# Mixing layer on one core: the last row tile of the output LayerNorm, with g multiplied early and the mean subtracted by TensorE

## The chip, the cores and the metric

The kernel runs on one core of one Trainium2 chip. The metric is the device time of one execution in microseconds, taken as the median of three executions. A further execution was profiled; its trace is what the rows below come from. Five engines work side by side and meet at semaphores: TensorE (PE in the rows, with its weight loads as PEld), VectorE (DVE), ScalarE (ACT), GpSimd (POOL) and SyncE (SP), which issues most DMA transfers. ScalarE issues some transfers too.

## The reference

One layer over a sequence of 1024 rows and a model width of 1024: an adaptive LayerNorm, one input projection, two groups of attention heads, one output projection, and a LayerNorm of the residual. What the change touches is the last line alone.

```python
u = _layer_norm(x) * (1.0 + scale) + shift
h = u @ w_in                              # q, k, v, gate path of both head groups
...                                       # forgetting attention, stick-breaking attention
y = concatenate([y_fox, y_sb]) @ w_out
resid = DEEPNORM_ALPHA * x + gate * y
x = _layer_norm(resid, ln_g, ln_b)        # (resid - mu) * rsqrt(var + 1e-5) * g + b
```

The mean and the variance are taken over the 1024 columns of a row, so no row can be finished before its last column group has come out of the output projection.

## The kernel before

**Tiles and stages.** The 1024 rows are eight tiles of 128 rows, one row per partition. The kernel normalises x, projects it, runs the eight pairs of heads, and multiplies the gated head outputs by w_out (already multiplied by the gate). TensorE's order is written out by hand; on the other engines the instructions go in the order in which a scheduler put them, one behind the other on each engine. Every product that needs more than the short format's precision is done as three products of rounded parts (a part "hi" and a rest "lo"), which is why lines 915, 916 and 917 always follow each other.

**The output stage.** `OUT_ORDER` takes the row tiles as 6, 7, 4, 5, 2, 3, 0, 1. `groups(t)` cuts the 1024 columns of a tile in two halves; the last tile, tile 1, is cut in three: group 0 with columns 0 to 511, group 1 with 512 to 767 and group 2 with 768 to 1023. For each group `o_step` runs eight steps of three products into a PSUM tile (`o` in the rows), and `o_half` takes it from there. The names in its rows:

- `xr` is the tile's part of x, `r` the tile's result in SBUF, which the stores read;
- `st_b` holds the statistics of each group (line 935), `mv_b` the mean and variance joined over all groups (line 189);
- `rs_b` is the reciprocal deviation, made on GpSimd in two steps from `mv_b` (lines 191 and 192);
- `lngb` holds g and b of the LayerNorm, spread over all partitions;
- `ident` is the 128 by 128 identity in 32 bits.

**The end of a tile.** Line 934 adds alpha x to the product, line 935 takes the statistics. After the last group come the joined mean and then two passes: `first` computes (value - mean) g, `second` multiplies by the deviation and adds b. For the first seven tiles VectorE does both. For the last tile the values stay in PSUM, all first passes are done on VectorE in the order group 1, 0, 2, and the second pass is shared out: `shared` multiplies by the deviation on ScalarE and adds b on GpSimd, for group 1 and the last 96 columns of group 2; VectorE does group 0 and the first 160 columns of group 2. ScalarE's queue then stores group 0 and SP's queue stores groups 1 and 2. Each store waits for every engine that wrote its columns.

**PSUM and its order.** A PSUM tile that several engines touch is ordered by the program's semaphores: where two engines read parts of one tile, the second waits for the first. The tag `S` holds a tile of two banks for attention scores, which is free once the attention is over; the tag `ty` holds 512 columns of SBUF per buffer, used by the head outputs.

Of the kernel before, what the change touches and what calls it, by code (L numbers as in the profile page):

```python
# [8 lines left out]
F32 = mybir.dt.float32  # L9
F32R = mybir.dt.float32r  # L10
AF = mybir.ActivationFunctionType
ALU = mybir.AluOpType

P = 128
SEQ = 1024
D = 1024
# [11 lines left out]
def tile_hybrid_layer(  # L28
# [17 lines left out]
    nc = tc.nc  # L46

    cp = ctx.enter_context(tc.tile_pool(name="const", bufs=1))
    sb = ctx.enter_context(tc.tile_pool(name="sb", bufs=1))
# [3 lines left out]
    def big(tag, bufs, name, dt=F32, shape=None):  # L53
        return sb.tile(shape or [P, 1024], dt, tag=tag, bufs=bufs, name=name)

    def att_tile(name, dt=F32):
        return big("att", 6, name, dt)
# [13 lines left out]
    def s_tile(name):  # L71
        return ps.tile([P, 2, 512], F32, tag="S", bufs=1, name=name)
# [17 lines left out]
    ident = cp.tile([P, P], F32, tag="ident", name="ident")  # L90
# [90 lines left out]
    for kt in range(NB):  # L181
        nc.tensor.matmul(sc_all[:, kt // 4, kt % 4 * P:][:, :P], sc[:, kt:kt + 1].to_broadcast([P, P]), ident,
                         start=True, stop=True)
# [3 lines left out]
    def ln_finish(st, name):  # L187
        mv = sb.tile([P, 2], F32, tag="mv", bufs=3, name=f"mv_{name}")
        nc.vector.bn_aggr(mv, st)
        rs = sb.tile([P, 2], F32, tag="rs", bufs=3, name=f"rs_{name}")  # L190
        nc.gpsimd.tensor_scalar_add(rs[:, 0:1], mv[:, 1:2], EPS)
        powed[0] = nc.gpsimd.tensor_tensor(rs[:, 0:1], rs[:, 0:1], mhalf, op=ALU.pow)
        return mv, rs
# [29 lines left out]
    def in_turn(make, *args):  # L223
        with after(*turn_of):
            turn_of[:] = [make(*args)]
        return turn_of[0]
# [456 lines left out]
    for kb in range(NB):  # L683
        last = kb == NB - 1
# [17 lines left out]
        else:  # L702
# [3 lines left out]
            rest = in_turn(u_rest, kb + 1)  # L706
# [107 lines left out]
    for kb in range(NB):  # L814
# [9 lines left out]
        if kb < len(evacs):  # L824
            n, h = evacs[kb]
# [5 lines left out]
    first = nc.scalar.copy(held[:, :512], acc1[0])  # L831
    last = nc.vector.tensor_copy(held[:, 512:], acc1[1])
# [46 lines left out]
    lgb = {}  # L879
# [21 lines left out]
    def groups(t):  # L901
        return ((0, 512), (512, 768), (768, 1024)) if t == OUT_ORDER[-1] else ((0, 512), (512, 1024))
# [18 lines left out]
    def o_half(t, h):  # L921
        ts_ = slice(t * P, (t + 1) * P)
        s = slice(*groups(t)[h])
        ng = len(groups(t))
        if h == 0:
            xr = big("k", 4, f"xr_{t}")
            nc.sync.dma_start(xr, x[ts_, :])
            res[t] = (att_tile(f"r_{t}"), xr, sb.tile([P, 3, 6], F32, tag="st", bufs=3, name=f"st_b{t}")[:, :ng, :])
        r, xr, st = res[t]
        last = t == OUT_ORDER[-1]  # L930

        acc = o_acc[t, h][:, :s.stop - s.start]
        to = acc if last else r[:, s]
        nc.vector.scalar_tensor_tensor(to, xr[:, s], ALPHA, acc, op0=ALU.mult, op1=ALU.add)
        nc.vector.bn_stats(st[:, h, :], to)
        if h == ng - 1:
            mv, rs = ln_finish(st, f"b{t}")
            cuts = [slice(*g) for g in groups(t)]
            mid = [o_acc[t, j][:, :c.stop - c.start] if last else r[:, c] for j, c in enumerate(cuts)]

            def first(j):
                nc.vector.scalar_tensor_tensor(mid[j], mid[j], mv[:, 0:1], lgb[0][:, 0, cuts[j]],
                                               op0=ALU.subtract, op1=ALU.mult)

            def second(c, m):
                nc.vector.scalar_tensor_tensor(r[:, c], m, rs[:, 0:1], lgb[0][:, 1, c], op0=ALU.mult, op1=ALU.add)

            def shared(c, m):
                nc.scalar.activation(r[:, c], m, AF.Copy, scale=rs[:, 0:1])
                nc.gpsimd.tensor_tensor(r[:, c], r[:, c], lgb[0][:, 1, c], op=ALU.add)  # L950

            if not last:
                for j in range(2):
                    first(j)
                    second(cuts[j], mid[j])
                    nc.sync.dma_start(out[ts_, cuts[j]], r[:, cuts[j]])
                return
            for j in (1, 0, 2):
                first(j)
            shared(cuts[1], mid[1])  # L960
            c = cuts[2]
            cut = c.stop - 96
            shared(slice(cut, c.stop), mid[2][:, cut - c.start:])
            second(cuts[0], mid[0])
            second(slice(c.start, cut), mid[2][:, :cut - c.start])
            nc.scalar.dma_start(out[ts_, cuts[0]], r[:, cuts[0]])
            rest = slice(cuts[1].start, c.stop)
            nc.sync.dma_start(out[ts_, rest], r[:, rest])

    def gen_out_first(t):  # L970
# [5 lines left out]
    def gen_out_last(t):  # L976
        for h in range(2):
            o_step(t, h, NPAIR - 1)
            o_half(t, h)
            yield  # L980

    def gen_out(t):
        for h in range(len(groups(t))):
            for pr in range(NPAIR):
                o_step(t, h, pr)
                if pr == NPAIR - 1:
                    o_half(t, h)
                yield
# [186 lines left out]
```

## Time and profile before

| what | value |
|---|---|
| median of 3 executions | 682.38 us (682.34 to 682.41) |
| profiled execution | 682.39 us, span of its trace 680.6 us |
| TensorE busy | 670.2 us (98% of the span) |
| VectorE busy | 484.8 us (71%) |
| GpSimd busy | 406.1 us (60%) |
| ScalarE busy | 380.1 us (56%) |
| granted TensorE clock, mean | 0.997 of full speed |
| the last 7.1 us of the span | from the end of TensorE's last product at 673.49 to 680.6, TensorE idle |

How to read it: the span runs from the first to the last event of the trace, and the execution's own time is 1.8 us longer. The times of rows are in microseconds from the span's start. A busy share is a mean over stages with different limits; what a change of the last tile can do is read from the last microseconds alone. The ends of products are modelled, since TensorE works on several at once: a product's row can be longer than the distance to the next one.

### The profile page before, as it was taken

How to read it: one execution, taken by the hardware profiler on the slowest of the kernel's cores; microseconds unless marked ns; L12 is line 12 of the kernel's file. 1: busy time of each engine (PE TensorE's matmuls, PEld its weight loads, DVE VectorE, ACT ScalarE, POOL GpSimd, SP SyncE). 2: the span in 40 equal slices, each digit the busy share in tenths (PEclk: the TensorE clock that was granted, in tenths of full speed). 3: DMA queues.
4: the chain of work that ended last, by engine and by line, in shares of the span. 5: the costliest groups of instructions: out<-in, count | busy, mean ns of one | idle time of the engine just before them, and what ended most of it. 6: DMA issues, size and time to landing. Idle time of an engine off the chain costs nothing.

```text
span 680.6 us, 11191 instructions
## 1 busy us (share of the span) xinstructions
PE 670.2 (98%) x3713; PEld 571.7 (84%) x3713; DVE 484.8 (71%) x996; ACT 380.1 (56%) x857; POOL 406.1 (60%) x530
## 2 busy tenths in 40 slices
PE   8999999999999999999999999999999999999995
PEld 5788898888997888889988888889988888888885
DVE  6787779868666777777676675766676777885645
ACT  6567368756566666666665564656565766521000
POOL 5550279756357656566369778786795365655412
PEclk9999999999999999999999999999999999999998
DMA  9983432112102122122134454363352297153301
GB/s 332 401 309 117 140 76 77 41 29 59 34 11 66 41 54 56 40 54 55 32 109 144 147 165 156 106 192 118 118 178 59 60 361 299 59 178 105 119 32 62
DMA packets 46472, 81.54 MB, mean 120 GB/s; under 512 B 5264, under 2 KB 20176, under 8 KB 46416
## 3 DMA queue, kind: packets, MB, share of 16 engines
q1 hardware_dynamic: 44832, 76.37, 34.6%
q10 hardware_dynamic: 1584, 4.47, 2.1%
q8 instruction: 29, 0.48, 0.3%
q14 instruction: 27, 0.22, 0.1%
HBM read 60.34 MB, written 16.29 MB: 113 GB/s over the span
## 4 chain that ended last, share of the span: by engine, by line
PE 94%; DVE 2%; ACT 1%; POOL 1%; issue 0%; POOLq 0%; DVEq 0%
PE m L297 10%; PE m L298 10%; PE m L299 10%; PE pv L531 10%; PE T L514 9%; PE S L463 5%; PE S L462 5%; PE o L917 4%; PE o L915 4%; PE o L916 4%; PE v L355 4%; PE v L357 4%; PE v L356 4%; PE st_late L623 1%; PE st_q L623 1%; PE sc_all L176 1%
## 5 line engine op out<-in xcount | busy, mean ns | idle before, releaser
L517 DVE TENSOR_TENSOR pt<-T,pt 128x512 fp32r<-128x512 f32 (+2 forms) x192 | 102.6, 553 | 43.2 <-ACT pt L516 41.7
L516 ACT CAST pt<-T 128x512 fp32r<-128x512 f32 (+2 forms) x192 | 88.7, 478 | 64.3 <-PE T L514 62.5
L297 PE MATMUL m<-uh,whi 128*128 128x512 f32 x304 | 123.4, 406 | 0.0
L299 PE MATMUL m<-uh,wlo 128*128 128x512 f32 x304 | 119.8, 394 | 0.0
L298 PE MATMUL m<-ul,whi 128*128 128x512 f32 x304 | 119.6, 394 | 0.0
L497 POOL TENSOR_TENSOR be<-be,kp 128x127 f32<-128x127 f32 (+3 forms) x64 | 79.0, 1235 | 37.4 <-DVE kp L495 25.8
L491 DVE TENSOR_TENSOR_SCAN kp<-kp,floor 128x512 f32<-128x512 f32 (+2 forms) x64 | 65.0, 1016 | 25.5 <-ACT kp L484 24.4
L531 PE MATMUL pv<-pt,v 128*128 128x512 f32 x320 | 82.8, 388 | 0.0
L478 POOL TENSOR_SCALAR a<-a,l 128x1024 f32<-128x1024 f32 (+3 forms) x64 | 48.4, 757 | 36.5 <-DVE l L476 27.8
L462 PE MATMUL S<-k,q 128*128 128x512 f32 (+5 forms) x192 | 68.8, 360 | 0.3 <-ACT be L486 0.3
L299 PEld LDWEIGHTS m<-uh,wlo 128*128 128x128 f32 x304 | 57.1, 188 | 13.7
L475 ACT ACTIVATE a<-a,nm 128x1024 f32<-128x1024 f32 (+3 forms) x64 | 49.8, 778 | 29.2 <-DVE nm L470 28.8
L297 PEld LDWEIGHTS m<-uh,whi 128*128 128x128 f32 x304 | 57.2, 188 | 10.1 <-PE T L514 0.3
L463 PE MATMUL S<-kl,qz 128*128 128x512 f32 (+5 forms) x192 | 65.3, 341 | 0.0
L298 PEld LDWEIGHTS m<-ul,whi 128*128 128x128 f32 x304 | 57.3, 188 | 9.0
L531 PEld LDWEIGHTS pv<-pt,v 128*128 128x128 f32 x320 | 55.4, 189 | 9.1
L547 POOL TENSOR_TENSOR ty<-ty,sg 64x256 f32<-64x256 f32 x64 | 47.0, 734 | 24.0 <-issue 11.0
L470 DVE CUSTOM_DVE_ANT_0 a<-S,fb 128x1024 f32<-128x1024 f32 (+3 forms) x64 | 48.2, 753 | 16.8 <-PE S L463 13.1
L436 ACT CAST qz<-q 64x128 fp32r<-64x128 f32 x128 | 37.3, 296 | 33.9 <-PE S L463 32.7
L355 PE MATMUL v<-whi_v,uh 128*128 128x256 f32 (+1 forms) x192 | 54.7, 285 | 0.0
L357 PE MATMUL v<-wlo_v,uh 128*128 128x256 f32 (+1 forms) x192 | 54.2, 282 | 0.0
L484 ACT ACTIVATE kp<-S 128x128 f32<-128x128 f32 (+3 forms) x64 | 42.0, 656 | 21.5 <-PE S L463 20.2
(289 smaller groups left out, 1622.6 us busy)
## 6 DMA issues: line engine op xcount, KB each, us to landing
raw<-in_w_qkg_dram SPq DMA_DIRECT2D x38, 256.0 KB, 2.8
wss<-in_w_ss_dram SPq DMA_DIRECT2D x16, 512.0 KB, 8.5
x<-in_x_dram SPq DMA_DIRECT2D x8, 512.0 KB, 6.6
k<-k SPq DMA_DIRECT2D x32, 128.0 KB, 2.3
wg<-in_w_gate_dram SPq DMA_DIRECT2D x8, 512.0 KB, 4.6
raw_o<-in_w_out_dram SPq DMA_DIRECT2D x16, 256.0 KB, 2.9
fb<-f_dr ACTq DMA_DIRECT2D x8, 512.0 KB, 4.4
wo_dr<-whi_o SPq DMA_DIRECT2D x16, 256.0 KB, 2.1
```

The source lines that it names most:

```text
L297: nc.tensor.matmul(acc, hi[:, c], u_hi[kt][:, s], start=(kt == 0), stop=False)
L298: nc.tensor.matmul(acc, hi[:, c], u_lo[kt][:, s], start=False, stop=False)
L299: nc.tensor.matmul(acc, lo[:, c], u_hi[kt][:, s], start=False, stop=(kt == NB - 1))
L355: nc.tensor.matmul(acc[:, :n], u_hi[kt][:, ts_], hi[:, s], start=(kt == 0), stop=False)
L357: nc.tensor.matmul(acc[:, :n], u_hi[kt][:, ts_], lo[:, s], start=False, stop=(kt == NB - 1))
L462: nc.tensor.matmul(S[:, s, :w], qst[p][h][:, qs], kst[p][h][:, ks], start=True, stop=False)
L463: nc.tensor.matmul(S[:, s, :w], z, klo[p][:, ks], start=False, stop=True)
L491: last_dve = nc.vector.tensor_tensor_scan(rv, rv, floor[:, :ke - lo], initial=0.0, op0=ALU.mult, op1=ALU.max)
L497: nc.gpsimd.tensor_tensor(be[:, :ke - 1], be[:, :ke - 1], kp[:, 1:ke], op=ALU.mult)
L516: nc.scalar.copy(hi[:, :n, qo:qo + P], t3)
L517: lows[:] = [nc.vector.tensor_tensor(lo[:, :n, qo:qo + P], t3, hi.bitcast(F32)[:, :n, qo:qo + P], op=ALU.subtract)]
L531: nc.tensor.matmul(acc2[:, :, q0:], vt[p][:, kb, h * P:(h + 1) * P], pt[:, :, q0:], start=(kb == 0), stop=(kb == last))
```

## The change

In the last tile alone, three things are different.

1. After the statistics of groups 0 and 1, VectorE at once writes value times g to `r` (line 937 of the changed kernel), before the mean is known.
2. TensorE multiplies these columns of `r` by the identity into `o_whole`, a tile of the two free banks of tag `S` (line 963). When the mean is there, VectorE makes a diagonal matrix of minus the mean, 128 by 128, in a buffer of tag `ty` (line 965), and TensorE adds the product of this diagonal and g to the same banks (line 967). The banks then hold value g - mean g, which is the result of `first`. For group 2 `first` stays on VectorE.
3. The second pass is shared out otherwise. `shared` takes group 1 in two pieces of 128 columns; VectorE does groups 0 and 2 whole.

```diff
         nc.vector.bn_stats(st[:, h, :], to)
+        if last and h < ng - 1:
+            nc.vector.tensor_tensor(r[:, s], to, lgb[0][:, 0, s], op=ALU.mult)
         if h == ng - 1:
             mv, rs = ln_finish(st, f"b{t}")
...
-            for j in (1, 0, 2):
-                first(j)
-            shared(cuts[1], mid[1])
-            c = cuts[2]
-            cut = c.stop - 96
-            shared(slice(cut, c.stop), mid[2][:, cut - c.start:])
+            whole = s_tile("o_whole")
+            mid[:2] = [whole[:, j, :c.stop - c.start] for j, c in enumerate(cuts[:2])]
+            for j in (0, 1):
+                nc.tensor.matmul(mid[j], ident, r[:, cuts[j]], start=True, stop=False)
+            dm = sb.tile([P, 512], F32, tag="ty", bufs=2, name="mean_diag")[:, :P]
+            nc.vector.tensor_scalar(dm, ident, mv[:, 0:1], -1.0, op0=ALU.mult, op1=ALU.mult)
+            for j in (0, 1):
+                nc.tensor.matmul(mid[j], dm, lgb[0][:, 0, cuts[j]], start=False, stop=True)
+            first(2)
+            for c in (slice(512, 640), slice(640, 768)):
+                shared(c, mid[1][:, c.start - cuts[1].start:c.stop - cuts[1].start])
             second(cuts[0], mid[0])
-            second(slice(c.start, cut), mid[2][:, :cut - c.start])
+            second(cuts[2], mid[2])
             nc.scalar.dma_start(out[ts_, cuts[0]], r[:, cuts[0]])
-            rest = slice(cuts[1].start, c.stop)
+            rest = slice(cuts[1].start, D)
             nc.sync.dma_start(out[ts_, rest], r[:, rest])
```

How the instructions stand on the engines is shown by the built programs. In their rows the operand left of the arrow is written, those right of it are read; the bracket names the semaphores waited for: `PE_49` is raised by TensorE, `DVE_49` by VectorE, `Activation_49` by ScalarE, `Pool_49` by GpSimd. `o_0`, `o_1` and `o_2` are the PSUM tiles of the three groups.

VectorE at the last tile, from group 1 to its end, before:

```order
L934 SCALAR_TENSOR_TENSOR o_1_7705<-xr_7699,o_1_7705 128x256 [waits PE_49]
L935 BN_STATS st_b_7702<-o_1_7705 128x6 [waits DVE_49]
L934 SCALAR_TENSOR_TENSOR o_2_7732<-xr_7699,o_2_7732 128x256 [waits PE_49]
L935 BN_STATS st_b_7702<-o_2_7732 128x6 [waits DVE_49]
L189 BN_AGGR mv_b_7759<-st_b_7702 128x2 [waits DVE_49]
L942 SCALAR_TENSOR_TENSOR o_1_7705<-o_1_7705,mv_b_7759,lngb 128x256 [waits DVE_49]
L942 SCALAR_TENSOR_TENSOR o_0_7674<-o_0_7674,mv_b_7759,lngb 128x512
L942 SCALAR_TENSOR_TENSOR o_2_7732<-o_2_7732,mv_b_7759,lngb 128x256
L946 SCALAR_TENSOR_TENSOR r_7701<-o_0_7674,rs_b_7761,lngb 128x512 [waits DVE_49,Pool_49]
L946 SCALAR_TENSOR_TENSOR r_7701<-o_2_7732,rs_b_7761,lngb 128x160 [waits Activation_49]
```

And now, from group 0's multiplication on:

```order
L937 TENSOR_TENSOR r_7701<-o_0_7674,lngb 128x512
L934 SCALAR_TENSOR_TENSOR o_1_7706<-xr_7699,o_1_7706 128x256 [waits PE_49]
L935 BN_STATS st_b_7702<-o_1_7706 128x6 [waits DVE_49]
L937 TENSOR_TENSOR r_7701<-o_1_7706,lngb 128x256
L934 SCALAR_TENSOR_TENSOR o_2_7734<-xr_7699,o_2_7734 128x256 [waits PE_49]
L935 BN_STATS st_b_7702<-o_2_7734 128x6 [waits DVE_49]
L189 BN_AGGR mv_b_7761<-st_b_7702 128x2 [waits DVE_49]
L965 TENSOR_SCALAR mean_diag<-ident,mv_b_7761 128x128 [waits DVE_49]
L944 SCALAR_TENSOR_TENSOR o_2_7734<-o_2_7734,mv_b_7761,lngb 128x256
L948 SCALAR_TENSOR_TENSOR r_7701<-o_2_7734,rs_b_7763,lngb 128x256 [waits DVE_49,Pool_49]
L948 SCALAR_TENSOR_TENSOR r_7701<-o_whole,rs_b_7763,lngb 128x512 [waits PE_49,Activation_49]
```

The second pass of group 0 moved behind that of group 2 and now waits for TensorE and for ScalarE; two multiplications stand ahead of the last group's statistics.

TensorE at its end, now (before, the program ended with line 917):

```order
L917 MATMUL o_2_7734<-wol_6735,y7h 128x256
L963 MATMUL o_whole<-r_7701,ident 128x512 [waits DVE_49]
L963 MATMUL o_whole<-r_7701,ident 128x256 [waits DVE_49]
L967 MATMUL o_whole<-lngb,mean_diag 128x512 [waits DVE_49]
L967 MATMUL o_whole<-lngb,mean_diag 128x256
```

Four 32-bit products came in behind the last step of the projection; in the built program TensorE's semaphore is raised once for the four, by the last.

ScalarE at its end, before:

```order
L949 ACTIVATE r_7701<-o_1_7705,rs_b_7761 128x256 [waits DVE_49,Pool_49]
L949 ACTIVATE r_7701<-o_2_7732,rs_b_7761 128x96 [waits DVE_49]
L966 DMA out_dram<-r_7701 128x512 [waits DMAHW7_49,DVE_49]
```

And now:

```order
L951 ACTIVATE r_7701<-o_whole,rs_b_7763 128x128 [waits DVE_49,PE_49,Pool_49]
L951 ACTIVATE r_7701<-o_whole,rs_b_7763 128x128
L973 DMA out_dram<-r_7701 128x512 [waits DMAHW0_49,DVE_49]
```

ScalarE's first piece now waits for TensorE too, and its store still waits for VectorE's second pass of group 0. On every engine the rows ahead of the last tile stand in the same order as before, with other line numbers.

## The prediction

> **What bounds the kernel now.** I read the page first, for the engine that carries the span.
>
> ```profile
> PE 94%; DVE 2%; ACT 1%; POOL 1%; issue 0%; POOLq 0%; DVEq 0%
> ```
>
> The chain that ended last is TensorE for 94% of it. The change touches no product of that part: it begins at the last row tile, so the question is what comes after TensorE's last product. I read that stretch in order of time (columns: start, duration, engine, line, operation, operands; in brackets the idle time before it and what ended it).
>
> ```profile
> 668.57 0.70 DVE L935 BATCH_NORM_STATS2 st_b<-o 128x6 f32<-128x512 f32 x1
> 670.69 0.43 DVE L934 SCALAR_TENSOR_TENSOR o<-xr,o 128x256 f32<-128x256 f32 x1 [1.42 <-PE o L917]
> 671.15 0.43 DVE L935 BATCH_NORM_STATS2 st_b<-o 128x6 f32<-128x256 f32 x1
> 673.21 0.28 PE L917 MATMUL o<-wol,y7h 128*128 128x256 f32 x1
> 673.52 0.43 DVE L934 SCALAR_TENSOR_TENSOR o<-xr,o 128x256 f32<-128x256 f32 x1 [1.94 <-PE o L917]
> 673.99 0.43 DVE L935 BATCH_NORM_STATS2 st_b<-o 128x6 f32<-128x256 f32 x1
> 674.46 0.24 DVE L189 BATCH_NORM_AGGREGATE mv_b<-st_b 128x2 f32<-128x18 f32 x1
> 674.73 1.54 DVE L942 SCALAR_TENSOR_TENSOR o<-o,mv_b,lngb 128x256 f32<-128x256 f32 x3
> 675.09 0.56 POOL L192 TENSOR_TENSOR rs_b<-rs_b,mhalf 128x1 f32<-128x1 f32 x1
> 675.68 0.96 ACT L949 ACTIVATE r<-o,rs_b 128x256 f32<-128x256 f32 x2 [47.03 <-POOL rs_b L192]
> 676.18 1.03 DVE L946 SCALAR_TENSOR_TENSOR r<-o,rs_b,lngb 128x512 f32<-128x512 f32 x2
> 676.23 1.07 POOL L950 TENSOR_TENSOR r<-r,lngb 128x256 f32<-128x256 f32 x2 [0.58 <-ACT r L949]
> 676.95 0.34 ACTq L966 DMA_DIRECT2D out_dram<-r  x1
> 677.33 0.33 SPq L968 DMA_DIRECT2D out_dram<-r  x1
> ```
>
> Three branches leave the mean at 674.70. GpSimd makes the reciprocal deviation by 675.65. VectorE runs three first passes until 676.27. ScalarE and GpSimd share the second pass with VectorE. ScalarE starts as soon as the deviation is there, because the first pass of group 1 went first and was done by 675.22. The two stores are issued at 676.95 and 677.33. The second waits for GpSimd, whose adds end at 677.30, while VectorE is done at 677.21: the branches are level within 0.1 us. A saving on VectorE alone is therefore worth nothing here.
>
> What follows the stores is shown by the windows (length, five busy times, granted clock, DMA share, GB/s).
>
> ```profile
> 677.70:678.00 0.30, 0.00 (x0) 0.00 (x0) 0.00 (x0) 0.00 (x0) 0.00 (x0) 0.50 0.64 246
> 678.00:678.30 0.30, 0.00 (x0) 0.00 (x0) 0.00 (x0) 0.00 (x0) 0.00 (x0) 0.50 0.98 375
> 678.90:679.20 0.30, 0.00 (x0) 0.00 (x0) 0.00 (x0) 0.00 (x0) 0.00 (x0) 0.50 0.78 294
> 679.20:679.50 0.30, 0.00 (x0) 0.00 (x0) 0.00 (x0) 0.00 (x0) 0.00 (x0) 0.50 0.01 0
> ```
>
> Data starts near 677.80, 0.85 us after the first issue, and fills the queues until 679.13 (1.33 us for both stores). The span ends 1.47 us later, at 680.6. The first store alone already has a share of 0.98, so the second adds to a queue that is full.
>
> **The change part by part.** Removed: two of the three first passes after the mean. Added on VectorE ahead of the mean: two multiplications by g, after the statistics of groups 0 and 1. They read PSUM with one more operand like line 934, so 0.70 us (its 512 wide form ran 0.70 too) and 0.43 us. The first would run from 669.3 to 670.0 and the second from 671.6 to 672.0. VectorE is idle there: 1.42 us before 670.69 and 1.94 us before 673.52. So they cost nothing; without that cover they would cost 1.13 us in front of the mean.
>
> Added on TensorE: two copies by the identity and two products by the diagonal, each 512 and 256 wide, all 32-bit on both sides. The nearest rows are the warm-up products of line 176, equal in type and width.
>
> ```profile
> 9.92 1.02 PE L176 MATMUL st_q<-ident 128*128 128x512 f32 x2
> 10.78 0.27 PE L242 MATMUL xT_early<-ident,x 128*128 128x128 f32 x1
> 12.07 0.60 PE L176 MATMUL st_q<-ident 128*128 128x256 f32 x2
> 12.51 0.27 PE L242 MATMUL xT_early<-ident,x 128*128 128x128 f32 x1
> ```
>
> One such product is two records. The 512 wide one holds the array 0.86 us (9.92 to 10.78), the 256 wide 0.44 us, and the last result comes 0.16 us after that. The copies go in behind line 917 at 673.33 and are through at 674.63, with results by 674.79. The mean is there at 674.70 and its diagonal later still, so TensorE's idle time hides them; without that cover they cost 1.30 us.
>
> The diagonal is new on the path. It is one 128 wide operation with a scalar per row, from SBUF to SBUF.
>
> ```profile
> L757 DVE TENSOR_SCALAR gate<-wg,sc 128x512 f32<-128x512 f32 x2 | 0.9, 480 | 0.0
> L217 DVE TENSOR_SCALAR x<-x,mv_a,rs_a 128x1024 f32<-128x1024 f32 x2 | 1.6, 814 | 0.6 <-POOL rs_a L192 0.5
> L842 DVE COPY floor<-ident 128x128 f32<-128x128 f32 x1 | 0.3, 289 | 0.0
> ```
>
> A line through 480 and 814 ns gives 0.23 us at 128; the copy of this size, into PSUM, took 0.29. I take 0.25: the diagonal is ready at 674.98.
>
> What a hand-over and a product after a wait cost is read here, the first three from the chain in order of time, the others from TensorE's first microseconds.
>
> ```profile
> 673.50 0.02 issue
> 674.70 0.08 issue
> 676.17 0.07 issue
> 13.67 0.50 PE L623 MATMUL st_q<-uh,whi_stk 128*128 128x512 f32 x1 [0.34 <-ACT uh L255]
> 14.01 0.40 PE L623 MATMUL st_k<-uh,whi_stk 128*128 128x512 f32 x1
> 14.24 0.39 PE L623 MATMUL st_g<-uh,whi_stk 128*128 128x512 f32 x1
> ```
>
> VectorE to GpSimd took 0.08, TensorE to VectorE 0.02; I take 0.07 to TensorE. The first product after a wait was followed 0.34 us later, the next 0.23 later, so 0.11 us of weight load is exposed. The products of the mean then run from 675.05: 0.11 + 0.86 + 0.60 = 1.57, to 676.62. No engine can start between the two, since the built program signals only behind the last: ScalarE and VectorE both wait for TensorE there.
>
> Here the stall is: ScalarE starts at 676.64 in place of 675.68, 0.96 us late, although the deviation was ready at 675.65 as before. The pieces that follow are shorter. Their prices lie between these groups:
>
> ```profile
> L949 ACT ACTIVATE r<-o,rs_b 128x256 f32<-128x256 f32 x1 | 0.5, 475 | 47.0 <-POOL rs_b L192 47.0
> L949 ACT ACTIVATE r<-o,rs_b 128x96 f32<-128x96 f32 x1 | 0.3, 342 | 0.1
> L950 POOL TENSOR_TENSOR r<-r,lngb 128x256 f32<-128x256 f32 x1 | 0.7, 725 | 0.6 <-ACT r L949 0.6
> L950 POOL TENSOR_TENSOR r<-r,lngb 128x96 f32<-128x96 f32 x1 | 0.4, 392 | 0.0
> L946 DVE SCALAR_TENSOR_TENSOR r<-o,rs_b,lngb 128x512 f32<-128x512 f32 x1 | 0.7, 743 | 0.0
> L942 DVE SCALAR_TENSOR_TENSOR o<-o,mv_b,lngb 128x256 f32<-128x256 f32 x2 | 1.0, 488 | 0.0
> ```
>
> At 128 wide that is 0.37 on ScalarE and 0.46 on GpSimd. ScalarE ends its first piece at 677.01 and its second, a little overlapped, at 677.33. GpSimd runs from 677.08; two pieces less the 0.05 by which the pair of before overlapped (0.725 + 0.392 against 1.07) are 0.87, to 677.95. SP issues its store at 677.98.
>
> VectorE is later still. It does the first and second pass of group 2 by about 676.2 (0.49 each, after 674.98), and then holds a new wait. The order shows its 512 wide second pass waiting for TensorE and for ScalarE: both of ScalarE's pieces read the same tile and stand ahead of it. It starts at 677.39 and ends at 678.13. Queued behind it is ScalarE's store of group 0, at 678.16; before, that store was the first to go, at 676.95.
>
> The sum: the first issue moves from 676.95 to 677.98, 1.03 us; the second from 677.33 to 678.16, 0.83 us. Both stores overlap as before, and one alone already fills the queues, so the end follows the first issue: 677.98 + 0.85 + 1.33 + 1.47 = 681.63 against 680.6, or +1.03 us. The page named Trainium Kernel Development and Optimization, in the Trainium skill, section Key Constraints, says that transfers issued from SP and ScalarE run on the same 16 DMA engines and interleave; the trace agrees, with a share of 0.98 for one store. By that rule the end follows the first issue, +1.03; if each store had a landing time of its own, it would follow the second, +0.83.
>
> The profiled execution took 682.39 (span 680.6 and 1.8 around it), 0.01 above the median of 682.38. The forecast is 682.39 + 1.03, so 683.4.
>
> Bounds: with the diagonal at 0.23, a hand-over of 0.02, no exposed load, ScalarE at 0.27 and GpSimd at 0.39 a piece, SP issues at 677.52: +0.57, 682.95. With 0.29, 0.08, a load of 0.19, no overlap of the two products (1.62), 0.40 on ScalarE and 0.48 on GpSimd, it issues at 678.41: +1.46, 683.85. I lie nearer the upper bound, by the rows of equal shape.
>
> **The rivals.** *The slow clock (slower).* If TensorE's clock falls to a half before the products of the mean, their 1.30 us of streaming double: +1.3 more, 684.7. These rows speak of it:
>
> ```profile
> 675.00:676.00 1.00, 0.00 (x0) 0.00 (x0) 1.00 (x3) 0.32 (x1) 0.56 (x2) 1.00 0.00 0
> 676.00:677.00 1.00, 0.00 (x0) 0.00 (x0) 1.00 (x3) 0.50 (x2) 0.77 (x2) 0.64 0.00 0
> ```
>
> The clock fell to 0.50 inside the second, about 2.8 us after the last product. After the change the gap is only 674.79 to 675.05, so it should stay up; it decides if the fall comes before 676. Falling at 676.3, as before, it doubles only the last 0.3 us. The Trainium skill, TensorE: Matmul & The Clock Gate, section What's actually happening, has the clock at a half after an idle window of about 3.4 us that runs free of the kernel. By that rule the products run at full clock and the sum stands at 683.4; the trace, with its fall after 2.8 us, neither needs nor excludes the window.
>
> *Cheap products.* If the 32-bit products cost as little as those of line 623 (0.23 us a 512 wide one, half of that a 256 wide), the chain shortens by 0.86 + 0.44 - 0.35 = 0.95 us and the end by as much: +0.1, 682.5. Against it stands line 176 with the same types on both sides. Even so nothing is gained, for ScalarE cannot start before 675.68 and VectorE still waits behind it.
>
> *A gain.* To end 1.4 us earlier, the first store would have to go at 675.6, before the deviation exists. I find no mechanism; what is left is chance of a different placement elsewhere, and the order shows no moved instruction ahead of the last tile.
>
> **How the numbers follow.** About 0.2%, 1.36 us, is what a measurement of this kernel can tell from no change, so slower begins at 683.74. The forecast has 73%, and its own range, 682.95 to 683.85, has about 11 of these above 683.74. The slow clock has 12%, cheap products 12%, a gain 3%. That makes faster 3%, same 62 + 12 = 74%, slower 11 + 12 = 23%. The range is 682.5 to 684.0: it takes in the cheap products and the bounds, and leaves out the gain and most of the slow clock.
>
> **What would show it.** Right: four 32-bit products behind line 917, the last two ending near 676.6; ScalarE's first piece at 676.6 released by TensorE and not by the deviation; VectorE's 512 wide second pass released by ScalarE at 677.4; the first store from SP near 678.0 and ScalarE's near 678.2; the clock at 1.00 to 676. Wrong: a mean product of 512 columns under 0.5 us, ScalarE released by GpSimd, VectorE's 512 wide pass beginning with ScalarE's, or the mean itself later than 674.7, which would mean that the multiplications or copies are not hidden.

## The result, and the profile after

The changed kernel takes 683.57 us against 682.43 us (medians of 18 runs each): a ratio of 1.0016, with a 95% interval of 1.0009 to 1.0023. It is 1.14 us slower: the interval does not hold 1. The median lies within the 0.2% (1.36 us) that the prediction set as the bound for no change; the interval's upper end lies a little beyond it. The forecast was 683.4. Of the 18 executions, which took 683.27 to 684.07 us, five spent 2.24 to 2.38 us outside the span in place of 1.8, and the profiled one (684.04) is among them, so what follows is read inside the trace.

The end of the changed kernel in order of time (start, duration, engine, line, operation, operands; in brackets the idle time before and what ended it):

```profile
669.46 0.67 DVE L937 TENSOR_TENSOR r<-o,lngb 128x512 f32<-128x512 f32 x1
670.96 0.43 DVE L934 SCALAR_TENSOR_TENSOR o<-xr,o 128x256 f32<-128x256 f32 x1 [0.83 <-PE o L917]
671.77 0.41 DVE L937 TENSOR_TENSOR r<-o,lngb 128x256 f32<-128x256 f32 x1
...
673.48 0.28 PE L917 MATMUL o<-wol,y7h 128*128 128x256 f32 x1
673.60 1.45 PE L963 MATMUL o_whole<-r,ident 128*128 128x512 f32 x4
673.80 0.43 DVE L934 SCALAR_TENSOR_TENSOR o<-xr,o 128x256 f32<-128x256 f32 x1 [1.62 <-PE o L917]
674.73 0.24 DVE L189 BATCH_NORM_AGGREGATE mv_b<-st_b 128x2 f32<-128x18 f32 x1
675.00 0.29 DVE L965 TENSOR_SCALAR mean_diag<-ident,mv_b 128x128 f32<-128x128 f32 x1
675.05 0.31 POOL L191 TENSOR_SCALAR rs_b<-mv_b 128x1 f32<-128x1 f32 x1 [8.98 <-DVE mv_b L189]
675.34 1.56 PE L967 MATMUL o_whole<-lngb,mean_diag 128*128 128x512 f32 x4 [0.29 <-DVE mean_diag L965]
675.45 0.56 POOL L192 TENSOR_TENSOR rs_b<-rs_b,mhalf 128x1 f32<-128x1 f32 x1
676.05 0.48 DVE L948 SCALAR_TENSOR_TENSOR r<-o,rs_b,lngb 128x256 f32<-128x256 f32 x1 [0.36 <-POOL rs_b L192]
676.99 0.62 ACT L951 ACTIVATE r<-o_whole,rs_b 128x128 f32<-128x128 f32 x2 [48.06 <-PE o_whole L967]
677.43 0.87 POOL L952 TENSOR_TENSOR r<-r,lngb 128x128 f32<-128x128 f32 x2 [1.42 <-ACT r L951]
677.65 0.75 DVE L948 SCALAR_TENSOR_TENSOR r<-o_whole,rs_b,lngb 128x512 f32<-128x512 f32 x1 [1.11 <-ACT r L951]
678.32 0.33 SPq L975 DMA_DIRECT2D out_dram<-r  x1
678.43 0.35 ACTq L973 DMA_DIRECT2D out_dram<-r  x1
```

Read the brackets. ScalarE's first piece is released by TensorE at 676.99, although the deviation (line 192) was there at 676.01. VectorE's 512 wide pass sits idle for 1.11 us and is released by ScalarE. Both waits are new.

In this trace TensorE's last projection product begins at 673.48, in that of before at 673.21, with the same instructions up to there. Over all the kernels below it lies between 673.01 and 673.48, though TensorE's order up to there is the same in all of them. The lowest value belongs to a kernel that has the early multiplications (early work alone), so the shift is not theirs. So positions are compared below as distances from the end of the joined mean (line 189), which is 674.97 here and 674.70 before; the mean itself comes 1.49 us after the start of the last product in both. By that measure ScalarE starts at 2.02 us after the mean (0.98 before), the first store goes at 3.35 (2.25) and the second at 3.46 (2.63).

The data of the two stores, in windows (length, five busy times, granted clock, DMA share, GB/s):

```profile
678.90:679.20 0.30, 0.00 (x0) 0.00 (x0) 0.00 (x0) 0.00 (x0) 0.00 (x0) 1.00 0.12 48
679.20:679.50 0.30, 0.00 (x0) 0.00 (x0) 0.00 (x0) 0.00 (x0) 0.00 (x0) 1.00 1.04 410
...
680.10:680.40 0.30, 0.00 (x0) 0.00 (x0) 0.00 (x0) 0.00 (x0) 0.00 (x0) 1.00 1.08 423
680.40:680.70 0.30, 0.00 (x0) 0.00 (x0) 0.00 (x0) 0.00 (x0) 0.00 (x0) 1.00 0.22 75
```

It runs from about 679.16 to 680.47, 0.84 us behind the first issue, without a gap, and the span ends at 681.8. From the mean to the end of the data it is 5.50 us, against 4.43 before: 1.07 us of the 1.14.

### The profile page after: what moved, and what is told of

It reads as the page before. It is cut to its first block, busy times and chain, and to the rows that moved or that the text cites. A ratio compares the mean times of both kernels' runs of the same rounds, so it can differ in the third digit from the quotient of the medians.

```text
span 681.8 us, 11209 instructions
## 1 busy us (share of the span) xinstructions
PE 672.6 (99%) x3721; PEld 572.8 (84%) x3721; DVE 485.3 (71%) x997; ACT 380.0 (56%) x857; POOL 405.8 (60%) x530
## 4 chain that ended last, share of the span: by engine, by line
PE 93%; DVE 3%; ACT 1%; DMA 1%; POOL 1%; issue 0%; SPq 0%; DVEq 0%; ACTq 0%; POOLq 0%
PE m L297 10%; PE m L298 10%; PE m L299 10%; PE pv L531 10%; PE T L514 9%; PE S L463 5%; PE S L462 5%; PE o L917 4%; PE o L916 4%; PE o L915 4%; PE v L355 4%; PE v L357 4%; PE v L356 4%; PE st_late L623 1%; PE st_q L623 1%; DMA x<-in_x_dram 1%
```

## The experiments

**One table for all.** Columns 2 to 4 are microseconds after the end of the joined mean in each kernel's own trace, worked out from its rows as above. "End" is what a count of the stores makes of columns 3 and 4, as a difference to the kernel before: the data ends 2.18 us after the first store (0.85 to the first data, 1.33 for both stores) or 1.52 us after the second (0.85 and half of 1.33), whichever is later, less the 4.43 of before. The first way of counting is the prediction's; the second is not in it, and was first used in the expectation for the two-tile kernel. "Measured" is the difference of the medians to the kernel before in the same comparison.

| kernel | ScalarE starts | first store | second store | end | measured |
|---|---|---|---|---|---|
| before | 0.98 | 2.25 | 2.63 | 0 | 0 |
| the change | 2.02 | 3.35 | 3.46 | +1.10 | +1.14 |
| mean products twice | 3.31 | 4.65 | 4.75 | +2.40 | +2.37 |
| two tiles | 2.02 | 2.32 | 3.35 | +0.44 | +0.52 |
| two tiles, group 1 first | 1.17 | 2.50 | 2.75 | +0.25 | +0.17 |
| rounded products | 1.14 | 2.48 | 2.59 | +0.23 | +0.14 |
| sharing alone | 0.98 | 2.26 | 2.68 | +0.01 | +0.01 |
| early work alone | 0.99 | 2.26 | 2.63 | +0.01 | 0.00 |
| rounded, two tiles, group 1 first | 1.15 | 2.32 | 2.48 | +0.07 | -0.02 |
| the same, VectorE's group 0 first | 1.14 | 1.95 | 2.48 | -0.30 | -0.35 |
| the same, diagonal from PSUM | 0.98 | 1.95 | 2.37 | -0.30 | -0.33 |
| the same, diagonal by ScalarE | 1.02 | 2.06 | 2.49 | -0.19 | -0.22 |

**Mean products twice.** Is the price that of TensorE's products on the path? Doubling them should add their streaming time, once.

```diff
-nc.vector.tensor_scalar(dm, ident, mv[:, 0:1], -1.0, ...)
+nc.vector.tensor_scalar(dm, ident, mv[:, 0:1], -0.5, ...)
+for j in (0, 1):
+    nc.tensor.matmul(mid[j], dm, lgb[0][:, 0, cuts[j]], start=False, stop=False)
 for j in (0, 1):
     nc.tensor.matmul(mid[j], dm, lgb[0][:, 0, cuts[j]], start=False, stop=True)
```

> The changed kernel with its two mean products done twice, each time with a diagonal of minus half the mean; the result is the same. Theory A (the 32-bit mean products stand on the path, and the stores follow them): the products stream 0.86 + 0.44 us more, ScalarE's first piece starts 1.30 us later after the joined mean (3.32 us in place of 2.02) and the time is 683.57 + 1.30 = 684.9 us. Theory B (the loss comes from the new sharing of the second pass, or from early work that is not hidden, and the products have cover): no change from 683.6. Theory C (the slow clock is what matters): a longer stretch of products, +2.6 us, 686.2.

684.64 us against 682.27 (ratio 1.0034, 1.0021 to 1.0046). The end in order of time:

```profile
674.45 0.24 DVE L189 BATCH_NORM_AGGREGATE mv_b<-st_b 128x2 f32<-128x18 f32 x1
...
676.46 1.45 PE L969 MATMUL o_whole<-lngb,mean_diag 128*128 128x512 f32 x4
678.00 0.63 ACT L951 ACTIVATE r<-o_whole,rs_b 128x128 f32<-128x128 f32 x2 [49.35 <-PE o_whole L969]
...
679.34 0.33 SPq L977 DMA_DIRECT2D out_dram<-r  x1
```

ScalarE starts 3.31 us after the mean, 1.29 later than in the change, and the time against the kernel before goes from +1.14 to +2.37. The products are on the path at their full length. No cover is left, and no effect of the clock appears: it is granted at 1.00 in every microsecond from 674 to 679.

**Two tiles.** Takes away VectorE's wait for ScalarE by giving group 1 a PSUM tile of its own. VectorE then does not wait for group 1's product either, since group 0's signals by itself; ScalarE still stands behind both products.

```diff
-mid[:2] = [whole[:, j, :c.stop - c.start] for j, c in enumerate(cuts[:2])]
+mid[:2] = [whole[:, 0, :512], pv_tile("o_one")[:, :256]]
```

> The changed kernel with the sums of groups 0 and 1 in two PSUM tiles in place of one, so that VectorE's 512 wide second pass no longer waits for ScalarE, and group 0's product signals by itself. Theory A (the products on the path, and VectorE's new wait delaying the store of group 0): ScalarE still starts 2.02 us after the joined mean and SP's store still goes at 3.35, but VectorE's 512 wide pass starts at about 1.5 in place of 2.68 and ScalarE's store goes at about 2.3 in place of 3.46. The data then ends 0.6 us earlier: 683.0 us, +0.5 to the kernel before. A rival, that VectorE's wait alone is the loss: back to 682.4. Another, that only the last store issued counts and the queues have room: the later store moves from 3.46 to 3.35, so 683.5.

682.79 us against 682.27 (1.0008, 1.0000 to 1.0017). In order of time, and then the windows of the stores:

```profile
674.33 0.24 DVE L189 BATCH_NORM_AGGREGATE mv_b<-st_b 128x2 f32<-128x18 f32 x1
...
675.91 0.59 PE L967 MATMUL o_one<-lngb,mean_diag 128*128 128x256 f32 x2
...
676.11 0.75 DVE L948 SCALAR_TENSOR_TENSOR r<-o_whole,rs_b,lngb 128x512 f32<-128x512 f32 x1
676.59 0.63 ACT L951 ACTIVATE r<-o_one,rs_b 128x128 f32<-128x128 f32 x2 [48.06 <-PE o_one L967]
676.89 0.34 ACTq L973 DMA_DIRECT2D out_dram<-r  x1
...
677.92 0.33 SPq L975 DMA_DIRECT2D out_dram<-r  x1
```

```profile
678.00:678.30 0.30, 0.00 (x0) 0.00 (x0) 0.00 (x0) 0.00 (x0) 0.00 (x0) 1.00 1.00 389
678.30:678.60 0.30, 0.00 (x0) 0.00 (x0) 0.00 (x0) 0.00 (x0) 0.00 (x0) 1.00 0.41 150
```

VectorE's pass no longer waits for ScalarE; group 0 is stored at 2.32 us in place of 3.46, and 0.6 us of the loss are gone. One store alone has a share of 1.00 in the first window, and it falls to 0.41 in the second: the first store's data is through before the second's begins, so from here the end hangs on the second store. That is where the two ways of counting the end part: 2.32 + 2.18 = 4.50, 3.35 + 1.52 = 4.87, and the measured +0.52 goes with 4.87. So the two waits of VectorE were worth 0.6 us of the 1.14. Nearly all of it belongs to the one for ScalarE: group 1's product ends at 676.50 by its row, so an estimate with that wait alone puts VectorE's start near 676.52, the first store at 2.73 and the end at +0.48 by the table's count, in place of +0.44. The rest stands with ScalarE's late start.

**Two tiles, group 1 first.** Of that rest, how much is the order of the products?

```diff
-for j in (0, 1):
+for j in (1, 0):
     nc.tensor.matmul(mid[j], dm, lgb[0][:, 0, cuts[j]], start=False, stop=True)
```

> As the two-tile kernel, with the mean product of group 1 ahead of that of group 0. Theory A: ScalarE no longer waits for the 512 wide product; it starts when the deviation is there, 1.05 us after the joined mean in place of 2.02, SP's store goes at 2.4 in place of 3.35, VectorE's 512 wide pass starts at 1.95 and ScalarE's store goes at 2.7. Against the kernel before (2.25 and 2.63) that is +0.1 to +0.2: 682.6 us. If the products cost less than 0.3 us of the path, the order would move nothing: 683.0 as with two tiles alone.

682.44 us against 682.27 (1.0002, 0.9993 to 1.0011).

```profile
674.30 0.24 DVE L189 BATCH_NORM_AGGREGATE mv_b<-st_b 128x2 f32<-128x18 f32 x1
...
675.71 0.63 ACT L951 ACTIVATE r<-o_one,rs_b 128x128 f32<-128x128 f32 x2 [47.21 <-PE o_one L967]
...
676.51 0.75 DVE L948 SCALAR_TENSOR_TENSOR r<-o_whole,rs_b,lngb 128x512 f32<-128x512 f32 x1 [0.41 <-PE o_whole L967]
677.04 0.33 SPq L975 DMA_DIRECT2D out_dram<-r  x1
```

ScalarE starts at 1.17 us, 0.85 earlier, nearly the 0.86 of the 512 wide product that no longer stands ahead of it. Of the 0.52 us left of the loss, 0.35 go with the order; the other 0.17 the interval does not tell from nothing. The expectation put ScalarE's start at 1.05; the product of group 1 still releases it, 0.13 after the deviation.

**Rounded products.** The change as it is, with one tile and both of its waits, but with cheap mean products. Left out is precision: g and the diagonal are rounded to the short format and no rest is added, so the mean's part is less exact. VectorE makes the rounded diagonal with another operation, which takes 0.35 us in place of 0.29.

```diff
+nc.scalar.activation(g_neg[0][:, 0, :], lgb[0][:, 0, :], AF.Copy, scale=-1.0)   # once, at group 0
...
-dm = sb.tile([P, 512], F32, tag="ty", ...)
-nc.vector.tensor_scalar(dm, ident, mv[:, 0:1], -1.0, op0=ALU.mult, op1=ALU.mult)
+dm = sb.tile([P, 512], F32R, tag="ty", ...)
+nc.vector.scalar_tensor_tensor(dm, ident, mv[:, 0:1], ident, op0=ALU.mult, op1=ALU.mult)
...
-    nc.tensor.matmul(mid[j], dm, lgb[0][:, 0, cuts[j]], start=False, stop=True)
+    nc.tensor.matmul(mid[j], dm, g_neg[0][:, 0, cuts[j]], start=False, stop=True)
```

> The changed kernel with the mean products in the rounded 32-bit format that the projection uses; what is left out is the precision of the mean's part: g (negated, copied once by ScalarE while it idles) and the diagonal are rounded, and no rest is added. One PSUM tile and VectorE's wait for ScalarE stay. Theory A (the price is the passes of full 32-bit products): 0.23 + 0.12 us of streaming in place of 0.86 + 0.44, so ScalarE starts when the deviation is there, 1.05 us after the joined mean in place of 2.02, the stores go at 2.4 and 2.5, and the time is +0.1 to +0.2 on the kernel before: 682.6 us. The rival, that VectorE's wait for ScalarE and the sharing are the loss: little gain, 683.2 to 683.6.

682.41 us against 682.27 (1.0001, 0.9992 to 1.0010).

```profile
675.10 0.62 PE L970 MATMUL o_whole<-g_neg,mean_diag 128*128 128x512 f32 x2 [0.36 <-DVE mean_diag L968]
...
675.80 0.63 ACT L954 ACTIVATE r<-o_whole,rs_b 128x128 f32<-128x128 f32 x2 [47.19 <-POOL rs_b L192]
...
676.46 0.75 DVE L951 SCALAR_TENSOR_TENSOR r<-o_whole,rs_b,lngb 128x512 f32<-128x512 f32 x1 [0.18 <-ACT r L954]
```

The two products take 0.62 us in place of 1.56, and ScalarE is released by the deviation again. With VectorE's wait and the sharing unchanged, the loss falls from 1.14 to 0.14 us, which the interval does not tell from nothing. VectorE still waits for ScalarE, but 0.18 us in place of 1.11. So most of what that wait cost came of ScalarE being late: it passed the products' price on to the store of group 0.

**Sharing alone, and early work alone.** Two parts of the change on the kernel before: the new sharing of the second pass; and the early multiplications with the copies by the identity, whose results are not used.

```diff
 # sharing alone
-shared(cuts[1], mid[1])
-shared(slice(cut, c.stop), mid[2][:, cut - c.start:])
+for c in (slice(512, 640), slice(640, 768)):
+    shared(c, mid[1][:, c.start - cuts[1].start:c.stop - cuts[1].start])
 second(cuts[0], mid[0])
-second(slice(c.start, cut), mid[2][:, :cut - c.start])
+second(cuts[2], mid[2])
 # early work alone
+if last and h < ng - 1:
+    nc.vector.tensor_tensor(r[:, s], to, lgb[0][:, 0, s], op=ALU.mult)
...
+whole = s_tile("o_whole")
+for j, c in enumerate(cuts[:2]):
+    nc.tensor.matmul(whole[:, j, :c.stop - c.start], ident, r[:, c], start=True, stop=True)
```

> The kernel before with only the new sharing of the second pass: ScalarE and GpSimd take group 1 in two pieces of 128 columns, VectorE takes groups 0 and 2 whole; the three first passes stay on VectorE. Theory A (the sharing is no part of the loss): GpSimd ends earlier and VectorE later, at 2.8 us after the joined mean in place of 2.5; the store of group 0 goes at 2.25 as before, that of SP at 2.83 in place of 2.63, and because the first store fills the queues the end stays: 682.4 us, within 0.2. Theory B (the sharing is the loss): +0.5 us or more. If the end follows the later store: +0.2.

> The kernel before with the early multiplications by g and the copies by the identity added, their results unused; the first and second passes stay as before. Theory A (this work lies in idle time): the joined mean comes as long after the last projection product as before (1.49 us from its start), the stores as before, 682.4 us within 0.2. Theory B (it is not hidden): up to 1.1 us more ahead of the mean if the multiplications are in the way, up to 1.3 if the copies are.

682.26 us with the sharing (1.0001, 0.9992 to 1.0009) and 682.25 with the early work (1.0000, 0.9991 to 1.0009), against 682.25. With the sharing the stores go at 2.26 and 2.68, as before within 0.05; VectorE's pair of second passes took 1.13 us in place of the 1.23 that the prediction's rows of 512 and 256 columns add up to (743 and 488 ns), so even the later store hardly moves. The sharing:

```profile
674.34 0.24 DVE L189 BATCH_NORM_AGGREGATE mv_b<-st_b 128x2 f32<-128x18 f32 x1
...
676.84 0.34 ACTq L964 DMA_DIRECT2D out_dram<-r  x1
677.26 0.33 SPq L966 DMA_DIRECT2D out_dram<-r  x1
```

With the early work, from its order of time:

```profile
673.01 0.28 PE L917 MATMUL o<-wol,y7h 128*128 128x256 f32 x1
673.13 1.45 PE L962 MATMUL o_whole<-r,ident 128*128 128x512 f32 x4
673.33 0.43 DVE L934 SCALAR_TENSOR_TENSOR o<-xr,o 128x256 f32<-128x256 f32 x1 [1.62 <-PE o L917]
...
674.26 0.24 DVE L189 BATCH_NORM_AGGREGATE mv_b<-st_b 128x2 f32<-128x18 f32 x1
```

The mean ends 1.49 us after the start of the last product, the same as without that work: the multiplications fall into VectorE's idle time, of which 1.62 us are still left, and the copies run beside the statistics. Neither part costs anything that the traces or the medians show.

**The parts put together.** If the products and the order of the stores are all that matters, cheap products with two tiles and group 1 first should come level with the kernel before, and VectorE doing group 0 ahead of group 2 should get ahead of it. Both have the rounded precision of the mean's part.

```diff
 # on top of the rounded products
-mid[:2] = [whole[:, j, :c.stop - c.start] for j, c in enumerate(cuts[:2])]
+mid[:2] = [whole[:, 0, :512], pv_tile("o_one")[:, :256]]
...                                          # mean products in the order (1, 0)
 # group 0 first
-second(cuts[0], mid[0])
-second(cuts[2], mid[2])
+with after(second(cuts[0], mid[0])):
+    second(cuts[2], mid[2])
```

> Rounded mean products, two PSUM tiles, group 1 first; the mean's part has the rounded precision. Theory A: ScalarE starts with the deviation at 1.05 us after the joined mean, SP's store goes at 2.4; VectorE does group 2 first, then group 0 from about 1.55 to 2.3, and ScalarE's store goes at 2.3. Against 2.25 and 2.63 before: the end follows the first store, so +0.1: 682.4 to 682.5 us. If the end follows the last store: -0.2.

> As the kernel with rounded products, two tiles and group 1 first, but VectorE's second pass of group 0 ahead of that of group 2. Theory A (the end follows the first store as long as it alone fills the queues): group 0 is done 1.85 us after the joined mean and stored at 1.87 in place of 2.25 before; SP's store goes at 2.4. The data ends 0.4 us earlier than before: 682.0 us. If the end follows the last store: 682.2. If the rounded products are still on the path: 682.6.

682.23 us (1.0000, 0.9991 to 1.0008) and 681.90 us (0.9995, 0.9986 to 1.0004) against 682.25. The second is the fastest kernel of the study, 0.35 us below the kernel before. Its interval holds 1, but its slowest execution (682.00) is below the fastest of the 33 of the kernel before beside it (682.05). Its order of time:

```profile
674.38 0.24 DVE L189 BATCH_NORM_AGGREGATE mv_b<-st_b 128x2 f32<-128x18 f32 x1
674.65 0.35 DVE L969 SCALAR_TENSOR_TENSOR mean_diag<-ident,mv_b 128x128 fp32r<-128x128 f32 x1
674.71 0.38 POOL L191 TENSOR_SCALAR rs_b<-mv_b 128x1 f32<-128x1 f32 x1 [8.98 <-DVE mv_b L189]
...
675.79 0.75 DVE L951 SCALAR_TENSOR_TENSOR r<-o_whole,rs_b,lngb 128x512 f32<-128x512 f32 x1 [0.38 <-POOL rs_b L192]
...
676.57 0.34 ACTq L977 DMA_DIRECT2D out_dram<-r  x1
677.10 0.33 SPq L979 DMA_DIRECT2D out_dram<-r  x1
```

Its second store goes as late as that of the kernel with VectorE's group 2 first (2.48 in both), and only the first moved, from 2.32 to 1.95: the time followed it by 0.33 us.

**Where the diagonal is made.** In these traces GpSimd's step of line 191 is longer than before (0.31 in the change, 0.38 here, 0.22 before). The row of the kernel before:

```profile
674.78 0.22 POOL L191 TENSOR_SCALAR rs_b<-mv_b 128x1 f32<-128x1 f32 x1 [8.98 <-DVE mv_b L189]
```

Two more kernels, on top of the last, ask whether VectorE's operation beside it is the reason.

```diff
 # diagonal from PSUM
+nc.scalar.copy(ident_ps[0], ident)          # once, at group 0
-nc.vector.scalar_tensor_tensor(dm, ident, mv[:, 0:1], ident, ...)
+nc.vector.scalar_tensor_tensor(dm, ident_ps[0], mv[:, 0:1], ident, ...)
 # diagonal by ScalarE
-nc.vector.scalar_tensor_tensor(dm, ident, mv[:, 0:1], ident, ...)
+nc.scalar.activation(dm, ident, AF.Copy, scale=mv[:, 0:1])
```

> The kernel with rounded products, two tiles and group 0 first, but VectorE makes the diagonal from a copy of the identity in PSUM, so that it reads one operand from SBUF in place of two. GpSimd's step of line 191 took 0.22 us in the kernel before and 0.38 beside the diagonal made from SBUF. Theory P (VectorE and GpSimd share a way to SBUF that VectorE's operation holds): line 191 back to 0.22 us, the deviation and all behind it 0.15 us earlier: SP's store at 2.33 us after the joined mean in place of 2.48, ScalarE's at 1.80 in place of 1.95, time 681.75 us against 681.9. Rival (GpSimd's step is longer because its own start or its operands differ): 0.38 stays, 681.9.

> The same, with the diagonal made by ScalarE, which idles there, in place of VectorE. Theory P: line 191 takes 0.22 us, since no VectorE operation with two SBUF operands runs beside it; the diagonal is ready about 0.35 to 0.4 us after the joined mean as before, ScalarE's first piece starts at 1.0 us in place of 1.14, SP's store goes at 2.33: 681.75 us. Rival: 0.38 stays and nothing moves, 681.9. If ScalarE's diagonal is slow (0.4 us or more), the products end at 1.1 and the deviation no longer binds: 681.85.

681.98 us (0.9996, 0.9988 to 1.0005) and 682.09 us (0.9996, 0.9987 to 1.0006) against 682.31; both intervals hold 1. The kernel with the diagonal from PSUM:

```profile
674.83 0.35 DVE L971 SCALAR_TENSOR_TENSOR mean_diag<-ident_ps,mv_b,ident 128x128 fp32r<-128x128 f32 x1
674.88 0.22 POOL L191 TENSOR_SCALAR rs_b<-mv_b 128x1 f32<-128x1 f32 x1 [8.98 <-DVE mv_b L189]
...
675.97 0.75 DVE L953 SCALAR_TENSOR_TENSOR r<-o_whole,rs_b,lngb 128x512 f32<-128x512 f32 x1 [0.39 <-PE o_whole L973]
```

Line 191 is back at 0.22 us beside an operation of VectorE as long as the other, and ScalarE starts 0.16 us earlier after the mean. The time expected from it, 0.15 us, did not come: VectorE's 512 wide pass now waits for the product (bracket), not for the deviation, so the first store stays at 1.95. The kernel with the diagonal by ScalarE:

```profile
674.59 0.22 POOL L191 TENSOR_SCALAR rs_b<-mv_b 128x1 f32<-128x1 f32 x1 [8.98 <-DVE mv_b L189]
674.60 0.40 ACT L969 ACTIVATE mean_diag<-ident,mv_b 128x128 fp32r<-128x128 f32 x1 [46.14 <-DVE mv_b L189]
```

It is the same there: 0.22 us for line 191, but a diagonal of 0.40 us and a first store at 2.06. So theory P holds for line 191, and its forecast of the time missed: a wait of nearly the same length stood behind the one removed.

## Why the prediction was right

The forecast was +1.03 us, for the reason that the end would wait for the mean's products; measured were +1.14.

- *Early work and copies at nothing*: right. The mean comes 1.49 us after the start of the last product with and without them.
- *The diagonal and the products*: 0.25 and 1.57 us were put in, 0.29 and 1.56 came. The warm-up products of the same type and width gave the price to 0.01. Doubling them moved ScalarE by 1.29, against 1.30 from the same rows.
- *Hand-overs*: TensorE to ScalarE was put at 0.02, from the row of VectorE's release; it took 0.09 (676.90 to 676.99). VectorE to TensorE was put at 0.07 and took 0.05. The first of these is the term that was mis-sized, together with 0.04 on the diagonal.
- *ScalarE's start*: 1.94 us after the mean was forecast, 2.02 came. SP's store 3.28 and 3.35; ScalarE's store 3.46 and 3.46. That the last agrees to 0.01 is luck: ScalarE started 0.08 later than forecast, and its two pieces took 0.62 us in place of 0.69.
- *The new wait of VectorE*, read from the order: it is there with 1.11 us. With two tiles 0.6 us come back, because the store of group 0 then goes 1.14 us earlier and the second store takes over.
- *The end follows the first store while one store fills the queues*: right to 0.1 us for every kernel in the table but the one with two tiles alone. There the stores lie 1.03 us apart, and the count from the second store, which the prediction did not have, comes within 0.1 us. The two together tie distances in a trace to the medians.
- *A saving on VectorE alone is worth nothing*: the sum does not use this remark, and it does not fit the rule above. It compares the branches at the second store (677.30 and 677.21). The first store, which the end follows, waited for VectorE's second pass of group 0 alone (676.18 + 0.74 = 676.92, issued at 676.95). In the two rounded kernels that differ only in VectorE's order, the time followed that pass by 0.33 us.
- *The mean not later than 674.7*: it ended at 674.97. The last projection product began 0.27 later too, so this was not the sign of uncovered work that the prediction meant it to be; the distance, 1.49 us, is the one to read.
- *The slow clock*: did not come. The granted clock is 1.00 in all windows of the products:

```profile
676.00:677.00 1.00, 0.90 (x4) 0.26 (x2) 0.48 (x1) 0.01 (x1) 0.01 (x1) 1.00 0.00 0
```

- *Cheap products bring no gain either*: forecast +0.1 for such a kernel, measured +0.14 with rounded products.

What the prediction missed is small and was covered: the deviation came at 1.04 us after the mean in place of 0.95, since GpSimd's step was held up; VectorE's second pass of group 2 waited 0.36 us for it, but the path went by the products, which ended at 1.93.

## What to carry to other kernels

Work taken off an engine is worth something only if what takes its place is shorter on the way to the event that bounds the end. Here that event was the first store: taking two passes from VectorE while putting 1.56 us of TensorE in front of both stores lost more than a microsecond, and the same idea with rounded products, two tiles and group 0 first came out 0.35 us ahead. Price a full 32-bit product from a row of its own type, look for who is signalled by the last of several products, and read from the order which engine waits because two operands share a tile. At the end of a program like this one, with two stores of 128 by 512 values each, count the data from the first issue while there is no gap between them, and from the last once there is; here that held to 0.1 us.

## What the runs showed of the hardware that was not expected

GpSimd's one-column step of line 191 took 0.22 us in the kernel before, 0.31 beside a 0.29 us operation of VectorE from SBUF to SBUF, 0.38 beside a 0.35 us operation with two operands in SBUF, and 0.22 beside the same operation with one operand in PSUM, or with the diagonal made by ScalarE. In the long cases it started 0.05 to 0.06 us after VectorE's operation and ended 0.07 to 0.09 us after it, which fits a step that is held until VectorE is done. The Trainium skill, SBUF — State Buffer, section Who interferes with whom, says that VectorE and GpSimd share a pair of ports to SBUF, that this pair is an exclusive lock, and that a VectorE instruction with two SBUF inputs contends there with a GpSimd instruction that reads SBUF, while one with at most one SBUF input does not unless it runs in a two-port mode. The traces agree: 0.38 with two inputs from SBUF, 0.22 with one of them in PSUM. That the 0.31 beside the one-input operation comes of a two-port mode is what the page would make of it; no run here separates it.
